# Two parts instead of chunk by chunk, and gate and up by Strassen's seven products

## The chip, the cores and the metric

The kernel runs on one core of a Trainium2 chip. The metric is the device time in microseconds (us). TensorE (PE in the profile) multiplies matrices, VectorE (DVE) and ScalarE (ACT) work on elements, GpSimd (POOL) and SyncE (SP) mostly issue transfers. Each engine works through its own queue of instructions in order and waits for the others at semaphores.

## The reference

One step of a streaming encoder of one layer, in float32: 2048 prompt tokens without history and 8 x 16 = 128 sample tokens with state, model width 1024, inner width of the FFN 2816.

```python
u = rms_norm(x, norm_mix) @ w_in
z, xbc, dt_raw, q, k, v, u_sc, u_cc = jnp.split(u, IN_SPLITS, axis=-1)
# four mixers: SSD scan, banded attention, short convolution, conformer convolution (31 taps)
mix = jnp.concatenate([ya, yb, yc, yd], axis=-1)
x = x + mix @ w_out
hf = rms_norm(x, norm_ffn)
x = x + (jax.nn.silu(hf @ w_gate) * (hf @ w_up)) @ w_down
y = rms_norm(x, norm_final)
```

Besides y the states, the last keys and values and the convolutions' histories are put out.

## The kernel before

**Layout.** Features lie on the 128 partitions and tokens along the columns. A matrix of 1024 features by T tokens is eight tiles [128, T]. The 2176 tokens are worked on in five chunks of 256, 512, 512, 512 (384 of the prompt and all 128 of the sample) and 384 tokens.

**Precision.** Every operand of a large matmul is split into a high and a low part in float32r. `split` (L177 to 179) makes the parts of an activation: a copy on ACT, a subtraction on DVE (L164, in the helper `tt`). `load_w` (L182) loads a weight block by a DMA on SP into one of three `wr` buffers (L191), copies it on ACT to `wh` (L192) and subtracts on DVE to `wl`. `group` (L198) then issues three matmuls for each contraction tile: wh x hi (L202), wh x lo (L203), wl x hi (L204), all summed in one PSUM bank `pm`.

**Stages of a chunk.** norm1 gives the operands `xn`. proj_in has 21 units; a unit loads one weight block of 1024 columns, makes 24 matmuls and hands the result to `after_in`. The mixers work from these tiles, mostly on DVE: the 31 taps of the long convolution are multiply-adds (`mix<-raw,tabh,mix`, helper `stt`, L167). proj_out has eight units that load an x tile, multiply, add, and sum squares. norm2 (L825) makes the operands `hf`. ffn (L839) has 22 tiles j of the inner width, each with a gate unit and an up unit of 24 matmuls, and for each round of j (4, 4, 4, 4, 3, 3) four down units, each for two of the eight output tiles, which add into `x2`. `final` normalizes and stores y (L894).

**Order.** `weave` (L905) runs a list of units and puts pieces of other work behind them at even distances; `run` binds each piece behind the last matmul so far. The mixers of the next chunk are spread over the first 85% of the units of this chunk's ffn, norm1 of the chunk after that over its middle, and norm2 lies beside the first units of proj_in of the next chunk. Weights and their splits have a higher priority, so that they run ahead as far as the buffers allow. Within these bounds a scheduler fixes each engine's queue when the kernel is built.

**Small matmuls.** Norms, attention and scan use short matmuls into the PSUM banks `px`, among them the sums of squares (L213) and the spreading of 1/rms over partitions (L231).

## Time and profile before

| what | us |
|---|---|
| median of 3 runs | 2435.03 |
| lowest, highest | 2432.83, 2435.9 |
| span of the profiled execution | 2430.4 |
| mean granted clock of TensorE | 0.997 |

The profile tells the busy time of each engine within its span, the same in forty equal slices, the DMA queues, and groups of equal instructions with their count and the mean duration of one. A view by form keeps different tile shapes apart. The timeline lists instructions with their start; for matmuls that are pipelined the distance of the starts, not the duration, is what one of them costs. A view by windows sums the busy times in a stretch of the span.

### The profile page before, as it was taken

Reading aid. Unit: us, or ns where it says so; the run is one execution under the profiler, and the core shown is the slowest. Engines: PE = TensorE matmul, PEld = TensorE weight load, DVE = VectorE, ACT = ScalarE, POOL = GpSimd, SP = SyncE. Lnnn points to the kernel's source line nnn. Section 1 sums busy time; section 2 is a strip of 40 time slices with the busy share of each in tenths; the row PEclk is TensorE's granted clock in tenths of the full one; section 3 lists DMA queues with packets and bytes.
Section 4 is the critical chain, followed back from the end, with each engine's and each line's share of the span. In section 5 each row is a group of like instructions: output and inputs, shape, how many; then the busy total and the mean of one; then the engine's idle time right before and its main releaser. Section 6 shows DMA issues by size and latency. Waiting matters only on the chain.

```text
span 2430.4 us, 32788 instructions
## 1 busy us (share of the span) xinstructions
PE 2386.1 (98%) x12701; PEld 2069.4 (85%) x12701; DVE 1648.1 (68%) x2997; ACT 919.5 (38%) x1460; POOL 86.3 (4%) x159
## 2 busy tenths in 40 slices
PE   7999999999999999999999999999999999999998
PEld 7888999888888888877788888889888888999997
DVE  8998998776975546675895455578864545475445
ACT  5544545444333333344333332334332323343332
POOL 1000000000000000001100000000000000000000
PEclk9999999999999999999999999999999999999999
DMA  6433444542222222353422222254322222343332
GB/s 234 135 117 131 158 155 152 199 157 100 90 92 87 87 91 89 137 167 92 135 96 87 87 87 92 91 191 125 112 87 87 90 94 96 133 152 123 131 119 98
DMA packets 106988, 290.78 MB, mean 120 GB/s; under 512 B 10848, under 2 KB 27456, under 8 KB 106832
## 3 DMA queue, kind: packets, MB, share of 16 engines
q1 hardware_dynamic: 102416, 276.34, 34.4%
q0 software_dynamic: 4416, 12.34, 1.6%
q8 instruction: 100, 1.64, 0.3%
q14 instruction: 56, 0.46, 0.1%
HBM read 277.93 MB, written 10.70 MB: 119 GB/s over the span
## 4 chain that ended last, share of the span: by engine, by line
PE 51%; DVE 1%; DMA 1%; issue 0%; ACT 0%; DVEq 0%; ACTq 0%; SPq 0%; POOLq 0%
PE pm L202 16%; PE pm L204 16%; PE pm L203 16%; PE px L231 0%; PE px L213 0%; PE px L640 0%; PE px L622 0%; PE px L650 0%; DMA x<-x 0%; PE px L549 0%; PE px L566 0%; DVE act L167 0%; DMA raw<-gst 0%; PE px L582 0%; DMA y<-x 0%
## 5 line engine op out<-in xcount | busy, mean ns | idle before, releaser
L202 PE MATMUL pm<-act,wh 128*128 128x512 f32 (+2 forms) x2920 | 1056.1, 362 | 3.6 <-ACT act L179 1.4
L204 PE MATMUL pm<-act,wl 128*128 128x512 f32 (+2 forms) x2920 | 1046.5, 358 | 10.8 <-DVE wl L164 10.8
L203 PE MATMUL pm<-act,wh 128*128 128x512 f32 (+2 forms) x2920 | 1045.5, 358 | 0.9 <-DVE act L164 0.9
L192 ACT ACTIVATE wh<-wr 128x1024 fp32r<-128x1024 f32 (+1 forms) x485 | 504.8, 1041 | 1193.8 <-PE pm L203 819.4
L164 DVE TENSOR_TENSOR wl<-wr,wh 128x1024 fp32r<-128x1024 f32 (+1 forms) x485 | 582.5, 1201 | 298.6 <-ACT wh L192 296.7
L204 PEld LDWEIGHTS pm<-act,wl 128*128 128x128 f32 x2920 | 551.8, 189 | 83.6 <-DVE wl L164 13.6
L202 PEld LDWEIGHTS pm<-act,wh 128*128 128x128 f32 x2920 | 551.6, 189 | 79.7 <-ACT wh L192 5.6
L203 PEld LDWEIGHTS pm<-act,wh 128*128 128x128 f32 x2920 | 552.2, 189 | 68.8 <-DVE act L164 1.3
L202 PE MATMUL pm<-h,wh 128*128 128x512 f32 (+2 forms) x880 | 317.7, 362 | 2.0 <-DVE ft L167 1.4
L203 PE MATMUL pm<-h,wh 128*128 128x512 f32 (+2 forms) x880 | 314.3, 357 | 0.0
L204 PE MATMUL pm<-h,wl 128*128 128x512 f32 (+2 forms) x880 | 314.0, 357 | 0.0
L167 DVE SCALAR_TENSOR_TENSOR ft<-ft,pm 128x512 f32<-128x512 f32 (+2 forms) x220 | 132.5, 602 | 166.2 <-PE pm L204 165.3
L164 DVE TENSOR_TENSOR x<-x,pm 128x512 f32<-128x512 f32 (+1 forms) x224 | 137.3, 617 | 134.7 <-PE pm L204 121.2
L167 DVE SCALAR_TENSOR_TENSOR mix<-raw,tabh,mix 128x384 f32<-128x384 f32 (+3 forms) x360 | 199.2, 589 | 1.9
L202 PEld LDWEIGHTS pm<-h,wh 128*128 128x128 f32 x880 | 165.8, 188 | 27.1 <-ACT wh L192 2.7
L203 PEld LDWEIGHTS pm<-h,wh 128*128 128x128 f32 x880 | 165.9, 189 | 20.9 <-issue 0.7
L204 PEld LDWEIGHTS pm<-h,wl 128*128 128x128 f32 x880 | 165.8, 188 | 20.8
L164 DVE TENSOR_TENSOR h<-ft,h 128x512 fp32r<-128x512 f32 (+2 forms) x110 | 66.8, 608 | 0.0
L179 ACT ACTIVATE h<-ft 128x512 fp32r<-128x512 f32 (+2 forms) x110 | 61.1, 555 | 5.3 <-DVE ft L167 4.5
L164 DVE TENSOR_TENSOR ns<-ns,nt 128x512 f32<-128x512 f32 (+2 forms) x91 | 56.9, 625 | 8.9 <-ACT nt L239 7.9
L164 DVE TENSOR_TENSOR act<-act,pm 128x384 f32<-128x384 f32 x56 | 30.9, 552 | 39.6 <-PE pm L204 39.6
L179 ACT ACTIVATE act<-nt 128x512 fp32r<-128x512 f32 (+2 forms) x72 | 40.2, 578 | 45.2 <-DVE nt L167 44.7
(219 smaller groups left out, 1338.6 us busy)
## 6 DMA issues: line engine op xcount, KB each, us to landing
wr<-w_gu SPq DMA_DIRECT2D x220, 512.0 KB, 3.2
wr<-w_in SPq DMA_DIRECT2D x105, 512.0 KB, 3.3
wr<-w_down SPq DMA_DIRECT2D x80, 512.0 KB, 3.4
wr<-w_out SPq DMA_DIRECT2D x40, 512.0 KB, 3.3
wr<-w_down SPq DMA_DIRECT2D x40, 384.0 KB, 3.1
nt<-x SPq DMA_DIRECT2D x48, 256.0 KB, 3.8
x<-x SPq DMA_DIRECT2D x24, 256.0 KB, 5.1
y<-x POOLq DMA_DIRECT2D x24, 256.0 KB, 4.4
```

Of the source, the lines that this page charges most:

```text
L164: return eng.tensor_tensor(out=out, in0=a, in1=b, op=op)
L167: return eng.scalar_tensor_tensor(out=out, in0=a, scalar=s, in1=b, op0=op0, op1=op1)
L179: act.activation(dst[:, 0, :n], src, AF.Copy)
L192: act.activation(hi[:, :n], rv, AF.Copy)
L202: pe.matmul(ps[:, :T], wh, o[:, 0, :T], start=(i == 0), stop=False)
L203: pe.matmul(ps[:, :T], wh, o[:, 1, :T], start=False, stop=False)
L204: mm = pe.matmul(ps[:, :T], wl, o[:, 0, :T], start=False, stop=(i == n - 1))
```

## The change

The program is cut in two. **Part one** runs norm1, proj_in, mixers and proj_out of all chunks; what proj_out makes (x + mix @ w_out) goes to a tensor `mid` in DRAM, by a DMA on POOL's queue. The mixers of a chunk are now woven into proj_out of the chunk before and proj_in of the chunk after. Tiles that live from one chunk to the next get two buffers.

**Part two** runs the FFN over three pairs of token blocks, 2 x 364, 2 x 362 and 2 x 362 tokens. All pools of part one are closed, and new ones take their place in memory. `prep` loads `mid`, sums the squares, loads `mid` again, scales, and builds for each of the four tiles of a contraction half the seven operands of Strassen's products, each split in two: 28 `hf` tiles. `quad_w` loads two weight blocks, and forms the seven weight operands from two tiles of the inner width and the two contraction halves. `quad` makes the seven products, each of 4 x 3 matmuls of N columns, in three PSUM banks, with copies and additions for the sums. Down is as before, but for the blocks of N tokens; the rounds are 4, 4, 4, 4, 4, 2.

```diff
-B = dict(wr=3, wh=2, wl=2, nt=4, b2=4, ut=3, raw=2, mix=4, h=5, ft=1)
+B = dict(wr=3, wh=2, wl=2, nt=4, b2=4, ut=3, raw=2, mix=5, act=17, u=2, x2=3)
+F = dict(g=8, h=5, wp=3, w1=2, fr=3)
...
-            sync.dma_start(x2[:, :T], x[:, m, o:o + T])
+            x2 = mk(np_, [P, TM], "x2", bufs=B["x2"])[:, :T]
+            sync.dma_start(x2, x[:, m, o:o + T])
             wh, wl = load_w(w_out[m], [KT, P])
             ps = mk(pm, [P, 512], "pm")
             group(ps, T, [(wh[:, k], wl[:, k], c["mix"][k]) for k in (4, 5, 2, 3, 0, 1, 6, 7)])
-            tt(x2[:, :T], x2[:, :T], ps[:, :T], ALU.add)
-            add_square(c["ss"], x2[:, :T], T, m == 0)
-            c["x2"].append(x2)
+            tt(x2, x2, ps[:, :T], ALU.add)
+            pool.dma_start(mid[:, m, o:o + T], x2)
...
-        units = ffn(c)
-        side = []
+        units, side = proj_out(c), []
+        if after:
+            side.append((twice(norm1(after)), 0, 4))
+            units += proj_in(after, W_IN_TILES)
...
         if nxt:
-            side.append((mixers(nxt), 0, int(len(units) * 0.85)))
+            side.append((mixers(nxt), 0, int(len(units) * 0.95)))
+        weave(units, *side)
+    first_part.close()
...
+    def prep(p):
+        N = p["N"]
+        for k in range(KT):
+            t = g_tile()
+            load_mid(p, k, t)
+            add_square_pair(p, t[:, :, :N], k == 0)
...
+        p["r"] = rstd_pair(p["ss"], N)
...
+        for i in range(4):
+            if rb is None:
+                rb = spread_pair(p["r"], N)
+            u = []
+            for k in (i, i + 4):
+                t = g_tile()
+                load_mid(p, k, t)
+                stt(t[:, :, :N], t[:, :, :N], T_("gffn", k), rb[:, :, :N], ALU.mult, ALU.mult)
+                u.append(t)
...
+            def put(n, src):
+                d = mk(xp, [P, 2, NB], "hf", F32R, bufs=28)
+                split(d, src, N)
+                p["X"][n][i] = d
+            put("11", b11)
+            put("21", b21)
+            put("22", b22)
+            tt(t1, b12, b11, ALU.subtract)
+            put("T1", t1)
+            tt(t2, b22, t1, ALU.subtract)
+            put("T2", t2)
+            tt(b12, b22, b12, ALU.subtract)
+            put("T3", b12)
+            tt(t2, b21, t2, ALU.subtract)
+            put("T4", t2)
...
+            da = split_w(r1, 1024)
+            tt(s1, a21, a22, ALU.add)
+            tt(s2, s1, a11, ALU.subtract)
+            ds = split_w(s_, 1024)
+            tt(a21, a11, a21, ALU.subtract)
+            dc = split_w(r2, 1024)
+            tt(a12, a12, s2, ALU.subtract)
+            d4 = split_w(a12, 512)
...
+        go(Z, 1, True)
+        act.activation(g1[:, 0, :N], Z[:, :N], AF.Copy)
+        go(Y, 2, True)
+        go(Z, 6, False)
+        act.activation(g1[:, 1, :N], Z[:, :N], AF.Copy)
+        tt(g1[:, 0, :N], g1[:, 0, :N], Y[:, :N], ALU.add)
+        go(V, 5, True)
+        act.activation(g2[:, 0, :N], V[:, :N], AF.Copy)
+        go(Z, 7, False)
+        act.activation(g2[:, 1, :N], Z[:, :N], AF.Copy)
+        go(V, 3, False)
+        tt(g2[:, 1, :N], g2[:, 1, :N], g2[:, 0, :N], ALU.add)
+        tt(g1[:, 1, :N], g1[:, 1, :N], V[:, :N], ALU.add)
+        go(Z, 4, False)
...
+    for t in twice(prep(pairs[0]), 7):
+        run(t)
+    for i, p in enumerate(pairs):
+        units = ffn(p)
+        n = len(units)
+        side = [(done, 0, 3)] if done else []
+        if i + 1 < len(pairs):
+            pr = twice(prep(pairs[i + 1]), 7)
+            side += [(pr[:3], n - 14, n - 9), (pr[3:], n - 9, n - 1)]
+        weave(units, *side)
+        done = twice(final(p))
```

**The border of the parts, SP.** Before there is no border. At the start of an FFN, here that of the second chunk, SP's queue goes from the weights of proj_in (`wr<-w_in`) straight to those of gate and up (`wr<-w_gu`), each waiting for a buffer that DVE gives free:

```order
L191 DMA wr_1848_10880<-w_in 128x1024 [waits DMAHW6_49,DMAHW3_49,DVE_49]
L191 DMA wr_1853_10913<-w_in 128x1024 [waits DMAHW4_49,DVE_49]
L191 DMA wr_1860_10955<-w_gu 128x1024 [waits DMAHW5_49,DVE_49]
L191 DMA wr_1867_10993<-w_gu 128x1024 [waits DMAHW6_49,DVE_49]
L191 DMA wr_1882_11081<-w_gu 128x1024 [waits DMAHW7_49,DVE_49]
```

With the change, the last x tiles of proj_out (`x2<-x`) are followed by the first weights of part two (`fr`) and by `mid` into the tiles `g`. DMASW are transfers on POOL's queue, that is, the stores to `mid`:

```order
L814 DMA x2_1543_8679<-x 128x384 [waits DMAHW4_49,DMASW3_49,DVE_49]
L983 DMA fr_1611_8940<-w_gu 128x1024 [waits DMAHW5_49,DMASW6_49,DVE_49]
L984 DMA fr_1612_8941<-w_gu 128x1024 [waits DMAHW6_49,DMASW4_49]
L983 DMA fr_1625_9065<-w_gu 128x1024 [waits DMAHW7_49,DMASW5_49]
L913 DMA g_1548_8742<-mid_87 128x728 [waits DMAHW0_49,PE_49,Activation_49]
L913 DMA g_1550_8746<-mid_87 128x728 [waits DMAHW1_49]
L984 DMA fr_1626_9066<-w_gu 128x1024 [waits DMAHW6_49,DMAHW2_49,DVE_49]
L983 DMA fr_1639_9191<-w_gu 128x1024 [waits DMAHW5_49,DMAHW3_49,DVE_49]
L913 DMA g_1552_8751<-mid_87 128x728 [waits DMAHW4_49]
L913 DMA g_1554_8756<-mid_87 128x728 [waits PE_49]
```

The weights and the operands of part two now stand behind the stores of part one, and six of the eight loads of `mid` stand behind two weight loads that wait for DVE.

**The making of the operands, DVE.** Before, norm2 of a chunk (scaled tiles `nt<-x2,tab,px` and low parts `act`) alternates on DVE with the weight splits `wl` of proj_in of the next chunk:

```order
L164 TENSOR_TENSOR wl_1759_10252<-wr_1757_10250,wh_1758_10251 128x1024 [waits DMAHW7_49,PE_49,Activation_49]
L164 TENSOR_TENSOR act_1737_10157<-nt_1736_10155,act_1737_10157 128x512 [waits Activation_49]
L167 SCALAR_TENSOR_TENSOR nt_1738_10160<-x2_1686_9859,tab_1_82,px_1731_10140 128x512
L167 SCALAR_TENSOR_TENSOR nt_1740_10165<-x2_1692_9896,tab_1_82,px_1731_10140 128x512 [waits DVE_49]
L167 SCALAR_TENSOR_TENSOR nt_1742_10170<-x2_1698_9933,tab_1_82,px_1731_10140 128x512 [waits DVE_49]
L164 TENSOR_TENSOR act_1739_10162<-nt_1738_10160,act_1739_10162 128x512 [waits Activation_49]
```

With the change, at the end of the first pair, the operands of the second (`g` scaled by `stt`, L174; sums and low parts `hf`, L171) alternate with the additions of the last down units into `x2`:

```order
L171 TENSOR_TENSOR x2_1708_9793<-x2_1708_9793,pg_2066_12889 128x364 [waits PE_49]
L174 SCALAR_TENSOR_TENSOR g_2069_12920<-g_2069_12920,tab_1_81,g_2043_12752 128x2x362 [waits DMAHW4_49]
L171 TENSOR_TENSOR hf_2071_12924<-g_2068_12917,hf_2071_12924 128x362 [waits Activation_49]
L171 TENSOR_TENSOR x2_1708_9793<-x2_1708_9793,pg_2067_12903 128x364 [waits PE_49]
L171 TENSOR_TENSOR hf_2072_12927<-g_2069_12920,hf_2072_12927 128x362 [waits Activation_49]
L171 TENSOR_TENSOR g_2070_12923<-g_2068_12917 128x362
L171 TENSOR_TENSOR w1024_2145_13311<-fr_2142_13306,w1024_2145_13311 128x1024 [waits DMAHW5_49,Activation_49]
L171 TENSOR_TENSOR hf_2073_12930<-g_2069_12920,hf_2073_12930 128x362 [waits Activation_49]
```

Norm2's two rows for a tile have become nearly seven, and they stand beside down units instead of proj_in.

**Within the FFN, DVE.** Before, a unit has one weight split and one or two rows of the gate:

```order
L167 SCALAR_TENSOR_TENSOR ft_2945_17593<-ft_2945_17593,pm_2944_17568 128x512 [waits Activation_49]
L167 SCALAR_TENSOR_TENSOR ft_2945_17593<-ft_2945_17593,pm_2951_17608 128x512 [waits DVE_49,PE_49]
L164 TENSOR_TENSOR wl_2960_17673<-wr_2958_17671,wh_2959_17672 128x1024 [waits DMAHW0_49,Activation_49]
L164 TENSOR_TENSOR h_2952_17634<-ft_2945_17593,h_2952_17634 128x512 [waits Activation_49]
L164 TENSOR_TENSOR wl_2965_17708<-wr_2963_17706,wh_2964_17707 128x768 [waits DMAHW1_49,PE_49,Activation_49]
```

With the change, sums of weights (`fs`, `fr`), four splits (`w1024`, `w512`) and the products' sums (`g`) stand there for two tiles:

```order
L171 TENSOR_TENSOR fs_1655_9320<-fs_1655_9320,fr_1653_9316 128x512 [waits DMAHW3_49,DVE_49]
L171 TENSOR_TENSOR fr_1654_9317<-fr_1653_9316,fr_1654_9317 128x512
L174 SCALAR_TENSOR_TENSOR g_1624_9058<-g_1624_9058,pg_1632_9086 128x364
L171 TENSOR_TENSOR h_1637_9185<-g_1623_9057,h_1637_9185 128x728 [waits Activation_49]
L171 TENSOR_TENSOR h_1638_9188<-g_1624_9058,h_1638_9188 128x728 [waits Activation_49]
L171 TENSOR_TENSOR g_1649_9215<-g_1649_9215,pg_1647_9213 128x364 [waits PE_49]
L171 TENSOR_TENSOR w1024_1656_9321<-fr_1653_9316,w1024_1656_9321 128x1024 [waits Activation_49]
L171 TENSOR_TENSOR fr_1653_9316<-fr_1653_9316,fs_1655_9320 128x512 [waits DVE_49]
L171 TENSOR_TENSOR w512_1659_9334<-fr_1653_9316,w512_1659_9334 128x512 [waits Activation_49]
L171 TENSOR_TENSOR w1024_1657_9326<-fs_1655_9320,w1024_1657_9326 128x1024 [waits Activation_49]
```

DVE's rows for weights have grown from one split a unit to four splits and four sums for two units of the same matrix.

More of the change, by code (lines that the diff above doesn't have):

```diff
@@ L67, in __init__ @@
         self.rounds = rounds
+        self.pairs = pairs
         self.np_tiles = sum(chunks)
@@ L933, in stream_step @@
         after = chunks[i + 2] if i + 2 <= last else None
-        done = (twice(final(chunks[i - 1])), 0, 2) if i else None
-        weave(proj_out(c), *([done, (twice(norm1(nxt)), 0, 3)] if i and nxt else []))
-        n2 = twice(norm2(c))
-        if nxt:
-            weave(proj_in(nxt, W_IN_TILES[0 if i else EARLY:]), (n2, 0, 2))
-        else:
-            weave(rest, (n2, 0, 2))
-        units = ffn(c)
-        side = []
-        if i == last - 1:
-            units, rest = units[:-4], units[-4:]
@@ new lines, in spread_pair, with load_mid @@
+    def spread_pair(r, N):
+        rb = g_tile()
+        bl = blocks_of(N)
+        for h in range(2):
+            pr = mk(py_, [P, 512], "py")
+            for i, b in enumerate(bl):
+                j = h * len(bl) + i
+                pe.matmul(pr[:, b:b + P], bc(r[:, j:j + 1], [P, P]), ident, start=True, stop=True)
+            act.activation(rb[:, h, :N], pr[:, :N], AF.Copy)
+        return rb
+    def load_mid(p, k, t):
+        N, o = p["N"], p["off"]
+        sync.dma_start(t[:, :, :N], mid[:, k, o:o + 2 * N].rearrange("p (h n) -> p h n", h=2))
@@ new lines, in stream_step, with product @@
+    XOF = {1: "11", 2: "21", 3: "22", 4: "T4", 5: "T1", 6: "T2", 7: "T3"}
+    def product(ps, N, w, xs, first):
+        wh, wl = w
+        n = len(xs)
+        for i, o in enumerate(xs):
+            a, b = o[:, 0, :N], o[:, 1, :N]
+            pe.matmul(ps[:, :N], wh[:, i], a, start=first and i == 0, stop=False, skip_group_check=True)
+            pe.matmul(ps[:, :N], wh[:, i], b, start=False, stop=False, skip_group_check=True)
+            mm = pe.matmul(ps[:, :N], wl[:, i], a, start=False, stop=(i == n - 1), skip_group_check=True)
+        tail[0] = mm.ins
@@ new lines, in quad, with go @@
+    def quad(p, w):
+        N, X = p["N"], p["X"]
+        Z, Y, V = (mk(pg, [P, 512], "pg") for _ in range(3))
+        g1, g2 = g_tile(), g_tile()
+        def go(ps, n, first):
+            product(ps, N, w[n], X[XOF[n]], first)
+        go(Z, 1, True)
[12 more added lines that the diff above has]
+        go(Z, 4, False)
+        return g1, g2, Z
@@ L952, in stream_step @@
+    for t in twice(prep(pairs[0]), 7):
+        run(t)
+    done = None
+    for i, p in enumerate(pairs):
[5 more added lines that the diff above has]
+            side += [(pr[:3], n - 14, n - 9), (pr[3:], n - 9, n - 1)]
         weave(units, *side)
-    for t in twice(final(chunks[last])):
+        done = twice(final(p))
+    for t in done:
         run(t)
```

271 lines of the change are left out of this document (163 added, 108 removed).

## Prediction

> **What bounds the kernel now.** I read the page first: its span, the busy times and two of the rows of forty slices (PE, then VectorE).
>
> ```profile
> span 2430.4 us, 32788 instructions
> PE 2386.1 (98%) x12701; PEld 2069.4 (85%) x12701; DVE 1648.1 (68%) x2997; ACT 919.5 (38%) x1460; POOL 86.3 (4%) x159
> PE   7999999999999999999999999999999999999998
> DVE  8998998776975546675895455578864545475445
> ```
>
> TensorE is the bound and waits 2430.4 - 2386.1 = 44.3 us in all. VectorE is near full while the mixers run, and half empty in the FFNs. A change that takes matmuls away gains their time, as long as it adds no new wait. So I need the price of a matmul by its columns, their number, and VectorE's prices. The timeline gives the interval between starts, as first and last row of unbroken runs: 30 rows of 512 columns, 77 of 384 and 29 of 256.
>
> ```profile
> 1505.36 0.39 PE L202 MATMUL pm<-act,wh 128*128 128x512 f32 x1
> ...
> 1511.93 0.39 PE L204 MATMUL pm<-act,wl 128*128 128x512 f32 x1
> 2379.68 0.33 PE L202 MATMUL pm<-h,wh 128*128 128x384 f32 x1
> ...
> 2392.86 0.33 PE L203 MATMUL pm<-act,wh 128*128 128x384 f32 x1
> 64.74 0.28 PE L203 MATMUL pm<-act,wh 128*128 128x256 f32 x1
> ...
> 68.10 0.28 PE L204 MATMUL pm<-act,wl 128*128 128x256 f32 x1
> ```
>
> 6.57 / 29 = 0.2266 us, 13.18 / 76 = 0.1734 us, 3.36 / 28 = 0.120 us: a straight line of 0.416 ns a column. On it 362 columns cost 0.1642 us and 364 cost 0.1651 us. Next the counts, in the groups by form (one third of each; L203 and L204 repeat L202's).
>
> ```profile
> L202 PE MATMUL pm<-act,wh 128*128 128x512 f32 x1752 | 691.8, 395 | 1.2 <-DVE x L164 0.9 <-ACT wh L192 0.3
> L202 PE MATMUL pm<-h,wh 128*128 128x512 f32 x528 | 208.2, 395 | 0.0
> ```
>
> A chunk has 21 x 24 = 504 matmuls of proj_in, 192 of proj_out, 44 x 24 = 1056 of gate and up, 528 of down; of act that is 1752 a chunk and of h 528, so three chunks of 512 columns have in each of the three lines 1752 and 528, as the rows say. The other chunks have 256 and 384 columns.
>
> **The matmuls.** Before, gate and up: 3168 x 0.2266 + 1056 x 0.1734 + 1056 x 0.120 = 1027.7 us; down by half of that, 513.9. After, a quad makes two tiles of 2N tokens in 7 x 4 x 3 = 84 matmuls of N columns; 22 quads a pair, so 1848 x 0.1651 + 3696 x 0.1642 = 912.0 us. Down has 1056 matmuls a pair: 174.3 + 346.8 = 521.1 us, 7.2 more, since short matmuls pay the line's constant more often. **TensorE saves 115.7 - 7.2 = 108.5 us**, if 362 columns lie on the line; the bounds are the neighbours' cost per column (0.1734 / 384 and 0.120 / 256): between 0.1635 and 0.170 us, a saving from 115 down to 58 us; I take the line, which three rows support. The instructions of after number 5544 and 3168, so the work does go. The Trainium skill's page "TensorE: Matmul & The Clock Gate", section "Back-to-back issue gap", gives an isolated gap of N/2.4 + 2.5 ns. By it the saving would be about 118 us, as an estimate. The trace does not agree: its rows stand 13.3 ns above N/2.4, and they decide.
>
> **VectorE's prices.** The last two groups, ft and ns, are the page's; the first seven are by form.
>
> ```profile
> L164 DVE TENSOR_TENSOR wl<-wr,wh 128x1024 fp32r<-128x1024 f32 x445 | 544.2, 1223 | 279.9 <-ACT wh L192 278.4
> L164 DVE TENSOR_TENSOR wl<-wr,wh 128x768 fp32r<-128x768 f32 x40 | 38.3, 957 | 18.7 <-ACT wh L192 18.3
> L164 DVE TENSOR_TENSOR x<-x,pm 128x512 f32<-128x512 f32 x168 | 115.0, 685 | 132.8 <-PE pm L204 119.7 <-DMA x<-x 12.9
> L164 DVE TENSOR_TENSOR act<-act,pm 128x384 f32<-128x384 f32 x56 | 30.9, 552 | 39.6 <-PE pm L204 39.6
> L164 DVE TENSOR_TENSOR h<-ft,h 128x512 fp32r<-128x512 f32 x66 | 45.3, 687 | 0.0
> L167 DVE SCALAR_TENSOR_TENSOR nt<-nt,tab,px 128x512 f32<-128x512 f32 x24 | 17.2, 742 | 2.3 <-DMA nt<-x 2.3
> L167 DVE SCALAR_TENSOR_TENSOR mix<-raw,tabh,mix 128x384 f32<-128x384 f32 x120 | 71.1, 611 | 0.6
> ...
> L167 DVE SCALAR_TENSOR_TENSOR ft<-ft,pm 128x512 f32<-128x512 f32 (+2 forms) x220 | 132.5, 602 | 166.2 <-PE pm L204 165.3
> L164 DVE TENSOR_TENSOR ns<-ns,nt 128x512 f32<-128x512 f32 (+2 forms) x91 | 56.9, 625 | 8.9 <-ACT nt L239 7.9
> ```
>
> From 552 to 685 ns is 1.04 ns a column: 0.53 us for 362 to 364 columns, 0.91 for 728, and 0.97 for a scalar_tensor_tensor of 728 with a table column.
>
> **Steady FFN.** A weight pair costs VectorE 3 x 1.223 + 5 x 0.687 = 7.1 us (splits and Strassen sums); with PSUM adds and the gate, a quad is about 11 us against 84 x 0.1642 = 13.8 us of matmuls. A round of four tiles with its down units is 57 us on VectorE and 86.7 on TensorE. The weights are read three times instead of five, and mid adds one store and two loads of the tokens, all on queues that TensorE doesn't wait for. So no wait here; if the weight buffers failed to keep ahead, 11 us would show in each quad. Copies from PSUM between products of one accumulator lie beside the product in between (12 x 0.1642 = 2.0 us).
>
> **Part one.** Here the FFN's cover goes: mixers must run beside projections alone. VectorE's FFN share was weights 300 x 1.223 + 40 x 0.957 = 405, ft 132.5, h 67, six sevenths of the x adds 144, two thirds of ns 38, norm and final steps about 72, in all 859. 1648 - 859 = 789 us stay for part one, against TensorE's 826 us: 677 of projections at the interval prices, and some 149 of the 167 us that the small matmuls hold (2386.1 less 2219 for all 11,400 large ones; the norms of the FFN have the rest, an estimate). Two windows bear on that, one where VectorE is full, and two at the sample tokens:
>
> ```profile
> 240.00:300.00 60.00, 60.00 (x499) 57.44 (x499) 59.18 (x120) 33.73 (x68) 2.90 (x4) 1.00 0.45 150
> 1080.00:1140.00 60.00, 54.38 (x232) 43.75 (x232) 37.81 (x71) 24.92 (x39) 7.64 (x9) 0.97 0.39 112
> 1140.00:1200.00 60.00, 56.30 (x242) 46.04 (x240) 48.50 (x106) 19.39 (x30) 8.45 (x14) 0.97 0.51 138
> ```
>
> VectorE can run at 59.18 of 60 us with TensorE never waiting, so a load of 95% can be carried; the 9.3 us lost at the sample tokens stay. The second set of buffers for the projection's tiles and the new weave are in this term too: I take **10 us** more for the imbalance of single stages (bounds 0 and 96 us, the latter if VectorE only reaches the 88% at which 789 takes 897, plus 25). The end is different: mixers of the last chunk have only eight proj_out units beside them (192 x 0.2266 and small matmuls, 56 us). By the order of VectorE behind the last proj_in weight there are 52 taps (31.8), 8 weight splits (9.8), 14 adds of 512 (9.6) and some 24 us of short rows: 75, and about 8 of latencies. **27 us** more (0 to 45).
>
> **The border.** SP's queue holds the first w_gu load behind the last store to DRAM, and the mid loads g behind it; the store and load prices are the DMA issues' medians. POOL's queue, 4% busy, takes 40 stores; a broadcast behind one waits at most for one unit, 5.4 us, which I cost at nothing (at most 10 us).
>
> ```profile
> wr<-w_gu SPq DMA_DIRECT2D x220, 512.0 KB, 3.2
> nt<-x SPq DMA_DIRECT2D x48, 256.0 KB, 3.8
> y<-x POOLq DMA_DIRECT2D x24, 256.0 KB, 4.4
> ```
>
> The chain: store 4.4, load 3.2, weight splits that must read the buffers before the next loads may go 7.1, the last g load with its square and add 5.5, rstd and spread 5.2 (the tail's rows below: 2.1 to the spread, 1.6 in it), then on VectorE 8 x 0.97 + 44 x 0.53 for the operands' sums and splits and 2.1 of weight sums, 33.2. Together 58.6; TensorE has 27 matmuls (4.5 us) meanwhile: **54 us** lost (25 if all operand work hid, 65 if SP's loads came late again). Before, norm2 lay under proj_in of the next chunk.
>
> **Two pair boundaries.** Operand tiles are all in use until a pair's last quad is done, so their rebuilding (31 us) meets the eight last down units: 192 x 0.1642 + 96 x 0.1642 = 47.3 us on TensorE, and on VectorE 31 + some 27 x 0.53 x2 adds + weights, squares and h 17: 62. **15 us** each, 30 (0 to 50).
>
> **Clock.** At the start eleven rows of 256 columns take twice the interval of those above:
>
> ```profile
> 18.59 0.41 PE L202 MATMUL pm<-act,wh 128*128 128x256 f32 x1
> ...
> 20.73 0.39 PE L204 MATMUL pm<-act,wl 128*128 128x256 f32 x1
> ```
>
> 2.14 / 10 = 0.214 us; from 17.33 to 20.9 that loses 1.8 us. With three waits long enough I take **5 us**. The clock-gate part of the same page of the Trainium skill (Part 1, "What's actually happening") has the clock halve after an idle window of some 3.4 us. By that, a boundary that starves in eight pieces would pay eight times, 14 us in all as an estimate; no row of before shows such pieces.
>
> **The tail** grows, since pair three ends with 724 columns where 384 stood:
>
> ```profile
> 2418.15 0.80 PE L213 MATMUL px<-con,ns 128*128 128x1 f32 x6 [2.17 <-DVE ns L164]
> 2421.07 1.62 PE L231 MATMUL px<-con,n 128*128 128x128 f32 x6 [2.12 <-DVE n L167]
> 2422.73 4.29 DVE L167 SCALAR_TENSOR_TENSOR act<-act,tab,px 128x384 f32<-128x384 f32 x8 [1.81 <-PE px L231]
> ```
>
> 8 final steps 4.3 to 7.7, squares and the copy of the spread 3, larger stores 2: **9 us** (4 to 14).
>
> **Sum.** Added: 10 + 27 + 54 + 30 + 5 + 9 = 135; saved 108.5; net +26.5 on the span, 2456.9. The median lies 4.6 us above the profiled span (2435.0 against 2430.4), so 2461.5, told as **2462 us, slower**.
>
> **Rivals.** *The forecast's own case, A*: added waits exceed the saving; 2432 to 2500 from the bounds; chance 0.62, of which 0.03 faster and 0.04 the same. *B, operands hide*: VectorE works off the operand rows beside the down units and the first products of the quad, so that 33 at the border and 30 at the boundaries go: 2462 - 63 = 2399. It decides the other way from 27 us hidden on. For it: the quads leave VectorE a fifth of its time. Against it: every product needs all four operand pieces, the last of them ready at the end of the rows. 2385 to 2438, chance 0.25, of which 0.04 the same. *C, VectorE becomes the bound of part one*: at 88% of its time, 789 gives 897 instead of 836, 61 more: 2523, 2500 to 2570; the full window speaks against it, the loss of the half empty FFN stretches for it. Chance 0.13. That the matmuls do not go is excluded by the count. A change under 0.2%, 4.9 us, cannot be told from none. Faster 0.21 + 0.03 = 0.24, the same 0.08, slower 0.55 + 0.13 = 0.68. From 2410 to 2525 leaves out about the lower 0.1 of B and half of C.
>
> **What will show it.** Right: matmul intervals of 0.164 us in the FFN; a stretch of some 50 us with TensorE nearly empty at about 870 us, two of 15 us some 490 us apart, VectorE full around them. A short stretch at the border (under 25 us) means B; TensorE slices of 8 through part one, with waits on VectorE's mix and wl, mean C. An interval at 362 columns off the line, or waits inside each quad for weights, would make the whole sum wrong.

## The result

The changed kernel takes 2494.09 us (median of 4 runs, 2493.64 to 2496.33) against 2435.23 us of the kernel before, beside which it ran: a ratio of 1.0242, with a 95% interval of 1.0227 to 1.0256. It is slower by 59 us, where the forecast was 26.5 us slower. The sign came out as forecast, and the time is lost at the places that the prediction names and at one more; the size is more than double.

The page of the changed kernel, its span, busy times, the slices of TensorE, VectorE and the granted clock:

```profile
span 2491.9 us, 34604 instructions
PE 2335.5 (94%) x13501; PEld 2184.6 (88%) x13501; DVE 1894.5 (76%) x3429; ACT 1028.8 (41%) x1689; POOL 97.5 (4%) x183
PE   7999999999998756999999989999999889999996
DVE  7998899888899847765667787666667876666665
PEclk9999999999999876999999989999999999999998
```

TensorE is idle for 2491.9 - 2335.5 = 156 us, where it was 44. The holes are seen in the slices: one around slices 13 to 16, two short ones at 24 and at 32 and 33. The clock falls in slices 14 to 16 and in 24. VectorE, which was half empty in the FFNs, now stands at 6 to 8 tenths in nearly all slices of part two.

A ledger says where the time went. For each matmul I take the distance to the next start, less what the prediction's line gives, (columns + 32) / 2.4 ns; what is left is time over the line, be it a wait, a halved clock or a dearer matmul. Before, the line's part is 2311 us and 109 are over it; after, 2202 and 279.

| place | over the line, after (us) | added | forecast |
|---|---|---|---|
| part one, to 911 us (before: all but the tail, 94.6) | 137.3 | 42.7 | 10 + 27 |
| border, 911 to 980 | 58.8 | 58.8 | 54 |
| two boundaries, 1430 to 1545 and 1930 to 2050 | 21.7 + 24.0 | 45.7 | 30 |
| the rest of the FFN | 14.6 | 14.6 | 0 |
| tail (before 14.4) | 22.8 | 8.5 | 9 |
| clock, in the places above | | | 5 |
| all | 279.1 | 170 | 135 |

The line's part fell by 109 us, as the count of matmuls said. The time over the line grew by 170 us instead of 135. Of the boundaries' 45.7, 15.0 and 14.8 us lie before 1500 and 2010 us, where the operands are rebuilt, and 6.8 and 9.2 behind, at the second quads.

Windows of the changed kernel: the end of part one, its last wait, the border, the first steady stretch and the first boundary. A row gives the stretch and its length, the busy us (and the instructions) of TensorE, its weight loads, VectorE, ScalarE and GpSimd, then the granted clock, the DMA engines' busy share and their GB/s.

```profile
700.00:800.00 100.00, 90.16 (x495) 81.44 (x493) 93.89 (x221) 47.19 (x90) 8.95 (x18) 0.95 0.31 97
860.00:880.00 20.00, 9.36 (x31) 7.38 (x32) 13.43 (x42) 4.56 (x10) 0.00 (x0) 0.50 0.00 1
920.00:940.00 20.00, 0.00 (x0) 0.00 (x0) 13.51 (x17) 7.97 (x10) 0.00 (x0) 0.50 0.61 221
940.00:960.00 20.00, 10.18 (x35) 8.42 (x36) 12.46 (x30) 6.31 (x13) 0.00 (x0) 0.50 0.36 104
1000.00:1100.00 100.00, 100.00 (x604) 100.00 (x604) 66.78 (x94) 39.28 (x56) 0.00 (x0) 1.00 0.24 74
1440.00:1460.00 20.00, 14.11 (x86) 13.81 (x84) 18.93 (x32) 9.39 (x14) 0.00 (x0) 0.90 0.42 142
```

From 920 to 940 us TensorE does nothing. In the steady FFN it never waits, and VectorE has a third of its time free. At the boundary VectorE is full and TensorE waits. The timeline of TensorE at the border (start, us, line, tiles, and in brackets the idle time before and its releaser):

```profile
911.37 0.34 PE L211 MATMUL pm<-act,wl 128*128 128x384 f32 x1
942.16 2.69 PE L895 MATMUL py<-con,g 128*128 128x1 f32 x12 [30.46 <-DVE g L171]
946.92 2.93 PE L907 MATMUL py<-con,n 128*128 128x128 f32 x12 [2.06 <-DVE n L174]
951.96 0.67 PE L1011 MATMUL pg<-hf,w 128*128 128x364 f32 x1 [2.11 <-ACT hf L186]
```

40.6 us lie between the last matmul of proj_out and the first product, and the products then come in pieces until 978 us. At the first boundary there are two waits, one in the down units and one in the second quad of the next pair, with the VectorE row behind which the second one stands:

```profile
1463.46 0.67 PE L1011 MATMUL pg<-h,w 128*128 128x364 f32 x1 [9.35 <-DVE x L171]
1520.83 0.69 DVE L171 TENSOR_TENSOR fs<-fr 128x512 f32<-128x512 f32 x1 [4.61 <-DMA fr<-w_gu]
1528.19 0.67 PE L1011 MATMUL pg<-hf,w 128*128 128x362 f32 x1 [4.62 <-ACT g L1032]
```

The first is the one of the prediction (additions into x2 behind operand rows). The second was not foreseen: a weight load comes late, then the sums, then the product.

### The profile page after: what moved, and what is told of

Same layout as the page of the kernel before. It is cut to its first block, busy times and chain, and to the rows that moved or that the text cites. A ratio compares the mean times of both kernels' runs of the same rounds, so it can differ in the third digit from the quotient of the medians.

```text
span 2491.9 us, 34604 instructions
## 1 busy us (share of the span) xinstructions
PE 2335.5 (94%) x13501; PEld 2184.6 (88%) x13501; DVE 1894.5 (76%) x3429; ACT 1028.8 (41%) x1689; POOL 97.5 (4%) x183
## 5 line engine op out<-in xcount | busy, mean ns | idle before, releaser
L1011 PE MATMUL pg<-hf,w 128*128 128x362 f32 (+1 forms) x1848 | 613.0, 332 | 20.6 <-ACT g L1032 11.3
L1012 PE MATMUL pg<-hf,w 128*128 128x362 f32 (+1 forms) x1848 | 610.3, 330 | 2.5 <-DVE hf L171 2.5
L1013 PE MATMUL pg<-hf,w 128*128 128x362 f32 (+1 forms) x1848 | 610.4, 331 | 0.0
L974 ACT ACTIVATE w<-fr 128x1024 fp32r<-128x1024 f32 (+1 forms) x270 | 252.1, 935 | 447.1 <-PE pg L1013 252.1
L209 PE MATMUL pm<-act,wh 128*128 128x512 f32 (+2 forms) x1160 | 425.1, 367 | 9.4 <-ACT act L186 4.9
L211 PE MATMUL pm<-act,wl 128*128 128x512 f32 (+2 forms) x1160 | 421.0, 363 | 1.1 <-DVE wl L171 1.1
L210 PE MATMUL pm<-act,wh 128*128 128x512 f32 (+2 forms) x1160 | 421.1, 363 | 0.1
L171 DVE TENSOR_TENSOR w<-fr,w 128x1024 fp32r<-128x1024 f32 (+1 forms) x270 | 288.4, 1069 | 132.6 <-ACT w L974 131.7
L1011 PEld LDWEIGHTS pg<-hf,w 128*128 128x128 f32 x1848 | 351.6, 190 | 25.8 <-ACT g L1032 12.7
L1011 PE MATMUL pg<-h,w 128*128 128x362 f32 (+1 forms) x1056 | 348.3, 330 | 18.7 <-DVE x L171 18.7
L1012 PEld LDWEIGHTS pg<-hf,w 128*128 128x128 f32 x1848 | 351.1, 190 | 4.6 <-DVE hf L171 4.1
L1013 PEld LDWEIGHTS pg<-hf,w 128*128 128x128 f32 x1848 | 352.1, 191 | 0.0
L1012 PE MATMUL pg<-h,w 128*128 128x362 f32 (+1 forms) x1056 | 348.5, 330 | 0.0
L1013 PE MATMUL pg<-h,w 128*128 128x362 f32 (+1 forms) x1056 | 347.8, 329 | 0.0
L209 PEld LDWEIGHTS pm<-act,wh 128*128 128x128 f32 x1160 | 221.3, 191 | 45.1 <-issue 6.9
L211 PEld LDWEIGHTS pm<-act,wl 128*128 128x128 f32 x1160 | 221.4, 191 | 30.8 <-issue 2.0
L210 PEld LDWEIGHTS pm<-act,wh 128*128 128x128 f32 x1160 | 221.4, 191 | 28.4 <-issue 1.7
L171 DVE TENSOR_TENSOR x<-x,pg 128x362 f32<-128x362 f32 (+1 forms) x288 | 150.4, 528 | 117.6 <-PE pg L1013 117.3
L1011 PEld LDWEIGHTS pg<-h,w 128*128 128x128 f32 x1056 | 200.1, 190 | 19.4 <-DVE x L171 19.3
L174 DVE SCALAR_TENSOR_TENSOR mix<-raw,tabh,mix 128x384 f32<-128x384 f32 (+3 forms) x360 | 206.7, 591 | 2.7
L1012 PEld LDWEIGHTS pg<-h,w 128*128 128x128 f32 x1056 | 200.1, 190 | 0.0
```

The source lines that it names most:

```text
L171: return eng.tensor_tensor(out=out, in0=a, in1=b, op=op)
L174: return eng.scalar_tensor_tensor(out=out, in0=a, scalar=s, in1=b, op0=op0, op1=op1)
L209: pe.matmul(ps[:, :T], wh, o[:, 0, :T], start=(i == 0), stop=False)
L210: pe.matmul(ps[:, :T], wh, o[:, 1, :T], start=False, stop=False)
L211: mm = pe.matmul(ps[:, :T], wl, o[:, 0, :T], start=False, stop=(i == n - 1))
L974: act.activation(d[:, 0], raw, AF.Copy)
```

## The experiments

Three theories stood against each other. **Parts**: the matmuls save what they should, and the two parts (border, end of part one) cost the rest. **Operands**: the making of Strassen's operands on VectorE costs it. **Matmuls**: a matmul of 362 columns is dearer than the line. Ratios are to the kernel before in the same job; its median there was 2435.7 to 2439.3 us. Part one of e3 is the changed kernel's, row for row, and ended at 921.5 instead of 911.4 us, so differences of some 10 us in part one between single profiles are not read.

**e1: Strassen undone, the parts kept.**

```diff
-        p["X"] = {n: [None] * 4 for n in ("11", "21", "22", "T1", "T2", "T3", "T4")}
+        p["X"] = {n: [None] * 4 for n in ("11", "12", "21", "22")}
...
-                d = mk(xp, [P, 2, NB], "hf", F32R, bufs=28)
+                d = mk(xp, [P, 2, NB], "hf", F32R, bufs=16)
...
-            g1, g2, Z = quad(p, quad_w(j, 0))
...
+            for h in range(2):
+                ps = mk(pg, [P, 512], "pg")
+                product(ps, N, (v[:, 0], v[:, 1]), p["X"][f"1{h + 1}"] + p["X"][f"2{h + 1}"], True)
```

> Two parts and three pairs as in the changed kernel, but gate and up without Strassen's products: 96 matmuls of N columns for two tiles and two blocks instead of 84, 16 operand tiles instead of 28, no sums of operands or weights. Theory (the products save what their count says, and the added waits belong to the two parts): gate and up go from 5544 to 6336 matmuls, +131 us at the 0.1658 us that a matmul of 362 or 364 columns takes in the trace; the making of the operands gets 28 rows of 0.53 us shorter, some 10 to 15 us at the border and up to 10 at each boundary: 2494 + 131 - 30 = 2595 us, 2575 to 2620. Rival (the quads have a cost of their own that eats the saving, in weights, PSUM copies or sums): under 2560.

2570.9 us, ratio 1.054 (1.0499 to 1.0581), between the two expectations: some 73 us above the changed kernel instead of 100. The ledger splits it. The line's part is 130 us longer, as expected. But 57 us over the line are gone, more than the 25 to 30 expected: at the border 26 of them (first product 30.8 us after the last proj_out matmul instead of 40.6, and then fewer pieces), and at the two boundaries and the quads behind them some 38, while the rest is some 7 longer. A window across its first boundary, and one in its steady FFN:

```profile
1440.00:1500.00 60.00, 60.00 (x370) 59.71 (x369) 44.24 (x79) 23.28 (x39) 0.54 (x1) 1.00 0.28 94
1000.00:1100.00 100.00, 100.00 (x604) 100.00 (x603) 34.90 (x49) 19.35 (x25) 0.00 (x0) 1.00 0.23 69
```

TensorE does not wait at all at this boundary. So the two parts with their blocks of 364 and 362 columns cost about 130 us against the kernel before, some 21 of them in the line's part, since there are more and shorter matmuls. Strassen's products win 130 us in matmuls and give 57 back in time over the line. Both Parts and Operands hold, with their shares. One thing is not told apart: twelve operand tiles fewer also leave other memory free. Of the 26 us at the border, some 17 are the pieces behind the first product, where operand rows are made; the 10 ahead of it can be the weight sums or that memory.

**e2: the pools of part two in another order.**

```diff
+    hp = ctx.enter_context(tc.tile_pool(name="hp", bufs=F["h"], reuse_waits="tile"))
+    rp_ = ctx.enter_context(tc.tile_pool(name="rp", bufs=KT, reuse_waits="tile"))
     xp = ctx.enter_context(tc.tile_pool(name="xp", bufs=1, reuse_waits="tile"))
     gp = ctx.enter_context(tc.tile_pool(name="gp", bufs=F["g"], reuse_waits="tile"))
     fw = ctx.enter_context(tc.tile_pool(name="fw", bufs=1, reuse_waits="tile"))
-    hp = ctx.enter_context(tc.tile_pool(name="hp", bufs=F["h"], reuse_waits="tile"))
-    rp_ = ctx.enter_context(tc.tile_pool(name="rp", bufs=KT, reuse_waits="tile"))
```

> Only the order in which the pools of part two are laid into memory is changed, so that the weight buffers and the tiles g lie where the mixers' tiles were, and the x2 and h tiles where proj_out works to the end. Theory (the 40 us from the last proj_out matmul to the first product are a chain of waits for memory that part one holds, and its loads, squares and weight splits can lie beside the last proj_out): the border goes from 59 us over the line to about 25, the total to 2460 us, 2450 to 2470. Rival (VectorE is the limit there anyway, and the work only moves): 2485 or more.

2482.36 us, ratio 1.0177 (1.0147 to 1.0206): 16 us better than the changed kernel by the ratios, half of what was expected. TensorE at the border:

```profile
924.38 0.34 PE L211 MATMUL pm<-act,wl 128*128 128x384 f32 x1
929.36 2.69 PE L895 MATMUL py<-con,g 128*128 128x1 f32 x12 [4.64 <-DVE g L171]
939.16 0.67 PE L1011 MATMUL pg<-hf,w 128*128 128x364 f32 x1 [2.11 <-ACT hf L186]
```

The 40.6 us have become 14.8, so 26 us of the chain of loads and squares were a wait for memory, as the theory has it. The pieces behind it remain: 26 us in which VectorE makes operands. In the ledger the border falls from 59 to 33 us, while part one ends at 924.4 instead of 911.4 us; that is partly the spread between profiles named above, and partly, it may be, work that only moved ahead of the border. Why the total gains 16 us and not 26 is not told apart.

**e3: the second loads of mid on POOL's queue.**

```diff
-        sync.dma_start(t[:, :, :N], mid[:, k, o:o + 2 * N].rearrange("p (h n) -> p h n", h=2))
+        (eng or sync).dma_start(t[:, :, :N], mid[:, k, o:o + 2 * N].rearrange("p (h n) -> p h n", h=2))
...
-                    load_mid(p, m, c)
+                    load_mid(p, m, c, pool)
```

> The second loads of mid, into x2, are issued on POOL's queue instead of SP's. Theory (early in pairs two and three SP stands at x2 loads that wait for the stores of y, and the weights of a quad wait behind them): the waits of 6.4 and 8.9 us at 1515 to 1545 and 2020 to 2050 us go, 2494 - 13 = 2481 us, 2476 to 2486. Rival (another wait comes last there, VectorE's or the x2 tiles themselves for the first down units): 2490 or more.

2500.73 us, ratio 1.0252 (1.0221 to 1.0283): nothing gained, the theory of SP's queue falls. Its timeline at the late weight, the issue on SP and the row that waits for it:

```profile
1518.53 0.33 SPq L984 DMA_DIRECT2D fr<-w_gu  x1
1527.88 0.69 DVE L171 TENSOR_TENSOR fs<-fr 128x512 f32<-128x512 f32 x1 [5.83 <-DMA fr<-w_gu]
```

The load is issued freely now and still takes 9.4 us, where the median of such loads is 3.5. Eight stores of y and eight loads of mid, 6 MB, move beside it.

**e5: these transfers spread, on e3.** The final norm of a pair comes in pieces of two tiles behind five units instead of three.

```diff
+            if k % 2 == 1 and k < 7 and p["i"] < len(cfg.pairs) - 1:
+                yield
...
-        side = [(done, 0, 3)] if done else []
+        side = [(done, 0, 5)] if done else []
...
-        done = twice(final(p))
+        done = twice(final(p), 5 if i + 1 < len(pairs) else 2)
```

> As e3 (second loads of mid on POOL's queue), and the final norm of a finished pair is cut into four pieces, put behind the first, second, third, fourth and fifth unit of the next pair, so that the eight stores of y and the eight loads of mid are spread over some 55 us instead of 15. Theory (e3 showed it: a weight load that takes 3.5 us takes 9 there, because 6 MB of stores and loads go beside it): the waits at the second quad of pairs two and three, 6.4 and 8.9 us, go: 13 to 15 us less than e3, ratio to before 1.0195. Rival (VectorE's final steps, not the transfers, set it): within 5 us of e3, ratio 1.024 or more.

2485.79 us, ratio 1.0203 (1.0173 to 1.0233): 12 us below e3 by the ratios. The window behind the second wait, the changed kernel's and then e5's:

```profile
1520.00:1540.00 20.00, 15.38 (x85) 15.08 (x84) 16.76 (x24) 6.76 (x11) 0.00 (x0) 0.91 0.39 132
1520.00:1540.00 20.00, 18.05 (x108) 17.46 (x107) 17.24 (x25) 9.07 (x14) 2.69 (x4) 1.00 0.59 190
```

TensorE is short by 2 us instead of 4.6, and its clock stays at 1.00. The load that came late takes 6.5 us at the first boundary instead of e3's 9.4, and VectorE waits 2.8 us for it instead of 5.8. So most of the second wait at a boundary was the collision of transfers; in the ledger some 10 us less than in e3 are over the line at the two boundaries. e5 spreads VectorE's final steps too, but the rows that waited had waited for the load.

**e4: matmuls that nobody reads, in the border's idle stretch.**

```diff
+    warm = mk(py_, [P, 512], "py")
+    for i in range(110):
+        pe.matmul(warm, ident, cn[:, :512], start=True, stop=True)
```

> 110 matmuls of 512 columns that nobody reads stand on TensorE between the last proj_out and the norm of the first pair, in the 30 us in which it is idle. Theory (the halved clock is a part of the border's price: 8.2 us of matmuls run at half speed from 917 to 978 us): a granted clock of 1.0 to the end of the idle stretch, and 4 to 8 us less, 2486 to 2490. Rival (the pieces of product one wait for their operands, so that their speed is hidden): within 2 us of 2494.

2566.26 us, ratio 1.0521 (1.049 to 1.0551). The filling was mis-sized: a float32 matmul of this size appears as two instructions, of 0.43 us each, so that 92 us were put where 30 were free. TensorE's row of these matmuls and two windows:

```profile
915.72 15.61 PE L1118 MATMUL py<-con 128*128 128x512 f32 x36
...
1000.00:1020.00 20.00, 14.79 (x51) 9.18 (x50) 7.08 (x20) 3.15 (x7) 0.00 (x0) 0.86 0.06 19
1020.00:1040.00 20.00, 11.00 (x28) 7.44 (x28) 19.61 (x39) 10.43 (x22) 0.00 (x0) 0.50 0.19 56
```

The total says nothing on the price, but the windows do on the mechanism: TensorE is busy up to 1007 us, and from 1020 to 1040, while operands come in pieces, the clock stands at 0.50 all the same. What halves it here is the thin stretch itself, not the idle one ahead of it.

**e6 and e7: work from VectorE to GpSimd.** e6 moves the low parts of four operands of seven, e7 every third low part of a weight of proj_in.

```diff
-        tt(dst[:, 1, :n], src, dst[:, 0, :n].bitcast(F32), ALU.subtract)
+        tt(dst[:, 1, :n], src, dst[:, 0, :n].bitcast(F32), ALU.subtract, eng)
...
-                split(d, src, N)
+                split(d, src, N, pool if n in ("11", "21", "22", "T1") else dve)
```
```diff
-            wh, wl = load_w(w_in[W_IN_TILES.index(name)], [KT, P])
+            wh, wl = load_w(w_in[W_IN_TILES.index(name)], [KT, P], pool if names.index(name) % 3 == 2 else dve)
```

> The low parts of four of the seven operands (16 of the 28 subtractions of a pair) go from VectorE to GpSimd. Theory (the making of Strassen's operands on VectorE sets the border's last 26 us and the 9.5 us waits of the down units at each boundary): 16 x 0.53 = 8.5 us less on VectorE at each of three places, so 9.5 us goes at each boundary and 5 to 8 at the border: some 25 us less, ratio 1.014. Rival (GpSimd is so slow at it, or slows VectorE so much, that operands come later than before): the waits stay or grow, ratio 1.024 or more.

> In part one every third low part of a weight of proj_in (35 of 105) goes from VectorE to GpSimd. Theory (VectorE is the limit at the end of part one, 93.9 of 100 us busy from 700 to 800, and its backlog is what TensorE waits for at 740 to 785 and 835 to 885, 50 us): 35 x 1.22 = 43 us less on VectorE, some 16 of them in the last 21 units; the two waits shrink by 10 to 20 us, ratio 1.018. Rival (those waits are chains of latency in the last steps of a chunk's mixers, not load): within 4 us, ratio 1.023 or more.

e6: 2514.15 us, ratio 1.0319 (1.0289 to 1.0349). e7: 2586.0 us, ratio 1.0614 (1.0583 to 1.0645). Both theories fall. e6's rival holds; e7's does not follow, since the kernel got 92 us slower instead of staying as it was. The rows by form of e6, GpSimd's and VectorE's, and of e7:

```profile
L171 POOL TENSOR_TENSOR hf<-g,hf 128x362 fp32r<-128x362 f32 x32 | 42.7, 1365 | 908.7 <-ACT hf L186 898.1 <-issue 10.6
L171 DVE TENSOR_TENSOR hf<-g,hf 128x362 fp32r<-128x362 f32 x24 | 17.4, 738 | 0.3
L171 DVE TENSOR_TENSOR g<-g,g 128x362 f32<-128x362 f32 x24 | 21.0, 893 | 0.0
```
```profile
L171 POOL TENSOR_TENSOR wl<-wr,wh 128x1024 fp32r<-128x1024 f32 x35 | 92.9, 2654 | 359.7 <-ACT wh L199 207.8 <-issue 38.7 <-ACT k L480 22.9
L174 DVE SCALAR_TENSOR_TENSOR mix<-raw,tabh,mix 128x512 f32<-128x512 f32 x120 | 100.2, 835 | 2.2
```

A subtraction of 362 columns takes 1365 ns on GpSimd instead of some 525 on VectorE, and the rows that stayed on VectorE grow too: hf to 738 ns, the sums of g to 893, and the taps of part one from 748 to 835. Not all do: the weight splits that e7 leaves on VectorE take 1235 ns instead of 1222. The Trainium skill, "GPSIMD Engine Reference", section "Specifications", says that GpSimd's SBUF interfaces are shared with VectorE and contend with its instructions that have two SBUF inputs; the stretched rows agree.

**e8: the matmul's price by itself.** Streams of 60 matmuls behind the end, in the pattern of a product.

```diff
+    for n in (512, 384, 368, 364, 362, 360, 352, 320, 256, 512):
+        ps = mk(pg, [P, 512], "pg")
+        for i in range(20):
...
+            pe.matmul(ps[:, :n], d[:, 0, a:a + P], d[:, 0, 512:512 + n], start=i == 0, stop=False, skip_group_check=True)
```

> The changed kernel with ten streams of 60 matmuls behind its end (512, 384, 368, 364, 362, 360, 352, 320, 256 and 512 columns, in the same pattern of weights and operands, nothing waited for, read by nobody). It measures by itself the interval that the prediction read off a line. Theory (the line is off by 1% between its points, for instance because the length is rounded up): 362 and 364 alike at 0.1655 to 0.166 us in a bare stream too. Rival (the line holds, 0.1642 and 0.1651, and the FFN's 0.1658 comes from small waits between its products).

First and last rows of the streams of 362 and 360:

```profile
2513.37 0.33 PE L1137 MATMUL pg<-w 128*128 128x362 f32 x1
...
2523.20 0.33 PE L1139 MATMUL pg<-w 128*128 128x362 f32 x1
2523.37 0.33 PE L1137 MATMUL pg<-w 128*128 128x360 f32 x1
...
2533.07 0.33 PE L1139 MATMUL pg<-w 128*128 128x360 f32 x1
```

The one run took 2575.45 us with the streams, and only they are read: 9.83 / 59 = 0.1666 us for 362 columns. The same reading gives 0.1666 for 364, 0.1668 for 368, 0.1644 for 360, 0.1610 for 352, 0.1737 for 384 and 0.1200 for 256. So 362 and 364 cost what 368 cost, 1.5 and 1% over the line, and the rival falls: the FFN's price is not one of small waits. The theory holds, with a figure a little above its 0.1655 to 0.166. Its reason, a length rounded up, is not shown: 368, 384 and 256 lie on the line, but 360 and 352 lie 0.7% above it as well (0.1633 and 0.1600), and they would have nothing to round at a step of 8. In the FFN 362 and 364 take 0.1658 and 0.1660 us by their starts, less than in the streams.

**e9: e2 and e5 together.**

> e2 and e5 together: the pools of part two in the other order, x2 loads on POOL's queue, final norms spread. Theory (they are separate waits at separate places, so they add): ratio to before 1.0177 - 0.004 = 1.0135, some 2470 us. Rival (one hides the other): 1.017 or more.

2461.52 us, ratio 1.0105 (1.0076 to 1.0134), 33 us below the changed kernel. The two add, and by the ratios there are 8 us more than their sum of 25.

**e10: chunks of 3, 4, 4, 3, 2 tiles, on e9.**

```diff
-    def __init__(self, chunks=(2, 4, 4, 3, 3), sample_in=3, ...
+    def __init__(self, chunks=(3, 4, 4, 3, 2), sample_in=3, ...
```

> e9 with chunks of 3, 4, 4, 3 and 2 tiles of the prompt instead of 2, 4, 4, 3 and 3: the last chunk, whose mixers have only eight proj_out units beside them, is a third smaller. Theory (the wait of 33 us at the end of part one is the excess of these mixers' 75 us of VectorE over 56 us of TensorE): the excess goes with 25 us less on VectorE, 15 to 25 us less than e9, against up to 8 more at the start, whose first chunk has 384 columns instead of 256. Rival (VectorE's backlog is that of all of part one, 95% full from 680 to 860 us, and is only moved): within 5 us of e9 or slower.

2487.82 us, ratio 1.0213 (1.0183 to 1.0243): 26 us above e9, as the rival has it, but the ledger puts them elsewhere. Part one has about as much over the line as in e9: its last wait falls from 33 to some 18 us, and new waits of 28 us come from 780 to 820. What is lost lies at the start, where the first matmul comes at 24.2 instead of 11.2 us, with the wider first chunk (13 us, 8 expected), and at the border (10 us more). VectorE is near full around the new waits:

```profile
700.00:800.00 100.00, 83.95 (x653) 73.82 (x652) 93.36 (x235) 51.33 (x108) 10.26 (x22) 0.94 0.41 133
800.00:900.00 100.00, 82.57 (x416) 66.57 (x416) 88.10 (x222) 35.13 (x74) 10.20 (x20) 0.86 0.31 103
```

So a smaller last chunk moves a part of the wait forward and does not shorten it in sum.

**e11: sums of squares on TensorE, on e9.**

```diff
-            tt(p["ss"][:, :, :N], p["ss"][:, :, :N], q[:, :, :N], ALU.add)
+                pe.matmul(p["pc"][:, i:i + 1], q[:, h, b:b + P], ones[:, 0:1], start=p["nk"] == 0, ...
```

> e9 with the sums of squares over the eight feature tiles made by TensorE (each square tile is multiplied by ones, summed in PSUM) instead of VectorE. Theory (VectorE is what the border and the boundaries wait for): 6.4 us less on VectorE for a norm, so up to 12.8 at each boundary, for 42 more short matmuls of some 0.1 us: the 9.5 us waits at each boundary shrink to under 3, 10 to 14 us less than e9. Rival (the waits come from the order on VectorE, operand rows and weight sums ahead of additions, and not from its load): within 4 us of e9.

2542.61 us, ratio 1.0438 (1.0408 to 1.0468). It does not make the reference's y, for a reason that stays open; the number and size of the instructions are those meant, and only they are read. My price for them was wrong:

```profile
L920 PE MATMUL py<-con,g 128*128 128x1 f32 x576 | 85.6, 280 | 1.5 <-ACT g L916 1.5
```

48 sums a norm appear as 96 instructions, 576 in six norms, and hold TensorE for 86 us. Nothing follows on what VectorE would have won.

**e12: additions into x2 first on VectorE, on e9.**

```diff
+                    with tc.high_priority(offset=2 * AHEAD):
                         tt(x2[:, h, :N], x2[:, h, :N], ps[:, :N], ALU.add)
```

> e9 with the additions of the down units into x2 ranked ahead of all else on VectorE. Theory (at a boundary the down units wait 9.5 us because operand rows and the next quad's weight sums stand ahead of the additions, but VectorE is loaded beyond TensorE there, 62 to 47 us, so that the wait only moves): the wait of the down units goes, one of the same size comes at the first quad, total within 4 us of e9. Rival (the order alone is at fault): some 20 us less than e9, ratio 1.003.

2459.73 us, ratio 1.0095 (1.0069 to 1.0122): within 2 us of e9. The wait of 9.35 us at the down units is gone, and at the first quad there are several small ones instead:

```profile
1438.80 0.44 PE L1011 MATMUL pg<-hf,w 128*128 128x362 f32 x1 [0.93 <-ACT hf L186]
1441.84 0.43 PE L1012 MATMUL pg<-hf,w 128*128 128x362 f32 x1 [1.05 <-DVE hf L171]
1443.58 0.67 PE L1011 MATMUL pg<-hf,w 128*128 128x362 f32 x1 [1.15 <-ACT w L974]
```

The theory holds for the most part: VectorE's load at a boundary makes the wait, not its order. Not wholly: in the ledger the two boundaries still fall from 37 us in e9 to 28, and the profiled run is the fastest of three (2453.79 us; the others took 2459.73 and 2460.65), so that some 8 us may belong to the order.

**e13 and e14: blocks of 368, 360 and 360 columns, on e9.** For the memory, e13 has seven tiles g, e14 one buffer for split weights of 512 columns.

```diff
-                 pairs=(364, 362, 362)):
+                 pairs=(368, 360, 360)):
...
-F = dict(g=8, h=5, wp=3, w1=2, fr=3)
+F = dict(g=7, h=5, wp=3, w1=2, fr=3)
```

> e9 with blocks of 368, 360 and 360 columns instead of 364, 362 and 362, and seven tiles g instead of eight, for the memory. Theory (a matmul pays for its columns rounded up to a multiple of 8, as the streams of e8 show: 0.1666 us at 362, 364 and 368, 0.1644 at 360): 5808 of the 8712 matmuls of the FFN get 0.0022 us shorter, 13 us less than e9, if seven tiles g do. Rival (seven tiles stall the products, or the FFN's interval does not follow the streams): e9 or slower.

> As e13, but with eight tiles g and one buffer for split weights of 512 columns instead of two. Theory as there: 13 us less than e9, less what the single buffer costs: each fourth product's weights can be split only when those of the last quad are used, 10 us ahead of need. Rival: the last down units of a pair, whose weights are 512 columns, wait for the one buffer, 4 x 1.5 us a pair, and e9 is not beaten by more than 4 us.

2458.99 us, ratio 1.0098 (1.0068 to 1.0127), and 2454.04 us, ratio 1.0087 (1.0051 to 1.0123). Steady stretches of 100 us, of the second pair in e13 and in the changed kernel, and of the first pair in e13 (the changed kernel's stands in the section on the result):

```profile
1600.00:1700.00 100.00, 100.00 (x615) 100.00 (x614) 68.38 (x96) 39.35 (x56) 0.00 (x0) 1.00 0.24 74
```
```profile
1600.00:1700.00 100.00, 100.00 (x605) 100.00 (x604) 65.70 (x93) 39.07 (x56) 0.00 (x0) 1.00 0.23 72
```
```profile
1000.00:1100.00 100.00, 100.00 (x598) 100.00 (x597) 66.74 (x94) 38.20 (x55) 0.00 (x0) 1.00 0.22 69
```

With 360 columns 615 matmuls fit in instead of 605: 0.1631 us instead of 0.1658 by the starts, a step like that of the streams. But with 368 columns 598 fit in instead of 604: 0.1678 us instead of 0.1660. So in the FFN 364 columns do not cost what 368 cost, as the expectation had it; what is left is 5808 x 0.0027 - 2904 x 0.0018, some 10 us. The medians lie 2.5 and 7.5 us below e9's, and that is not clear of the runs' spread (e14: 2452.43 to 2462.11), so neither the 13 us nor the rivals are decided. No kernel of the study is faster than the one before.

## Why the prediction came out as it did

**The count and the line.** The matmuls went as counted, and the line's part fell by 109 us against 108.5. But the FFN's matmuls take 0.1658 us by their starts, not 0.1642 and 0.1651: 8712 x 0.1658 = 1444 us against 1541.6 before, a saving of 97. I let three rows at 256, 384 and 512 columns support a straight line for 362; e8 finds these three on the line and 352, 360, 362 and 364 above it. The prediction's own upper end, 0.170, held the value, and an interval off the line was among its signs of a wrong sum; the choice between the ends was wrong by 11 us, and the ledger books 14.6 in the row of the rest of the FFN.

**Part one.** 43 us instead of 37. Its cause is the rival C in mild form: VectorE is at 93.89 of 100 us from 700 to 800, and TensorE loses 17 us at 740 to 785, besides the 33 at the end of part one (27 forecast). How much of the waits is VectorE's load and how much a chain of short steps was e7's question, which slowed VectorE instead. For the last wait the trace tells it:

```profile
848.11 1.19 PE L660 MATMUL px<-b,vt 128*64 128x256 f32 x8
851.88 10.42 DVE L174 SCALAR_TENSOR_TENSOR mix<-raw,tabh,mix 128x384 f32<-128x384 f32 x16
862.95 1.65 PE L733 MATMUL px<-ut,con 128*128 128x384 f32 x2 [13.65 <-DVE ut L171]
877.81 1.01 PE L209 MATMUL pm<-act,wh 128*128 128x384 f32 x2 [3.86 <-ACT act L186]
```

In the first 14 us VectorE works off the last taps without a pause, so that is load. The 16 us behind them are the chain of the long convolution's norm, with VectorE busy for 13.43 of 20 us and the clock at 0.50: there the steps wait for one another, for which the prediction had set apart 8 us. For 740 to 785 us it stays open.

**The border.** 59 us against 54. The chain was as written, 40.6 us to the first product and then operand pieces; e2 shows that its first part is a wait for memory, and e1 that some 17 us of the pieces, and with less certainty 10 us ahead of them, belong to Strassen's operands.

**The boundaries. The step that failed most**: "15 us each, 30" became 45.7. VectorE's load of 62 us against 47 of TensorE was right, in kind (for the most part, by e12) and in size: 15.0 and 14.8 us in the ledger, though partly by luck, since some 2.5 of each are the halved clock. But the step stopped there and put what follows at nothing. Behind it, the stores of y and the reloading of mid meet the weights of the second quad, and a load of 512 KB takes 7.6 and 8.6 us there instead of 3.5 (e3 and e5); this stretch adds 6.8 and 9.2 us, 16 in all, of which e5 takes 10 away. I had priced those transfers by their number, on "queues that TensorE doesn't wait for", and had not looked at when they go.

**The clock.** 5 us were set apart for three restarts. The mean granted clock is 0.966 instead of 0.997; outside of the start and the end, some 150 us of the changed kernel are at half clock, and TensorE is idle for about half of them. At the boundaries the price can be read, since TensorE has no more waits just behind the long one:

```profile
1463.93 0.51 PE L1012 MATMUL pg<-h,w 128*128 128x364 f32 x1
...
1466.96 0.51 PE L1013 MATMUL pg<-h,w 128*128 128x364 f32 x1
```

3.03 / 10 = 0.30 us instead of 0.166, until 1469.7 us. By the starts, the stretches at half clock behind the four waits of the boundaries lose some 7.5 us together, as an estimate; they are a part of the 45.7, so this term was too small. At the border the pieces from 952 to 978 us run at a clock of 0.50, and e4 shows the same behind a busy stretch; what that costs could not be told apart from VectorE's pace. The prediction named a rule of the Trainium skill ("TensorE: Matmul & The Clock Gate", Part 1, "What's actually happening"): the clock halves after an idle window of some 3.4 us, so that each piece that starves would pay. The trace agrees for the four waits at the boundaries, of 4.6 to 9.4 us, behind which the clock stands at 0.50 for a while; the pieces at the border stay at 0.50 although no idle time between them is above 3.3 us.

**The tail**, 8.5 against 9, was right. Rival B, at a chance of 0.25, did not come: the operands were not hidden at the border, and at the boundaries no more than the prediction had it.

The sum is a difference of two numbers above 100, and 35 us of error together (16 at the second quads, 15 in the price of a matmul, the rest at the end of part one and the border, less the 5 booked for the clock) more than doubled a net of 26.5.
